# Even mixer's two borders: where the second stack, the gates' transposition, the context's norm and the late squares are issued

## The chip, the cores and the metric

The kernel runs on one core of one Trainium2 chip. The metric is device time in microseconds (us) of one execution, the median of several. The core's engines run side by side and each takes its own instructions in order: PE (TensorE) multiplies matrices and transposes, DVE (VectorE), ACT (ScalarE) and POOL (GpSimd) work on elements, and SP issues transfers from HBM.

## The reference

The program is a two-layer backbone over 256 context tokens and 256 latent tokens of width 1024. Layer 0 is a feed-forward, a mixer and a second feed-forward; layer 1 is the same with another mixer. The change lies in layer 0's ("even") mixer: differential attention with four heads beside a bidirectional mLSTM with four heads, which share one input and one output projection. Cut to what the change touches:

```python
def mlstm_scan(q, k, v, ig, lf, state):          # per direction, in chunks
        bcum = jnp.cumsum(fc, axis=-1)           # running sum of the log forget gates
        dmat = jnp.where(tril, bcum[..., :, None] - bcum[..., None, :] + ic[..., None, :], -jnp.inf)
        m_t = jnp.maximum(m_inter, jnp.max(dmat, axis=-1))
        s = jnp.einsum('bhtd,bhsd->bhts', qc, kc) * jnp.exp(dmat - m_t[..., None])
        num = jnp.einsum('bhts,bhse->bhte', s, vc) + ...
        h = num / jnp.maximum(jnp.abs(den), jnp.exp(-m_t))[..., None]

def ada_norm(x, g, shift, scale):                # ahead of every mixer and feed-forward
    return rms_norm(x, g) * (1.0 + scale) + shift

        x = x + mx[:, 5] * yx                    # residual behind the mixer, latents
        hctx = hctx + mc[5] * yc                 # and context
        x = x + 0.5 * mx[:, 8] * swiglu(ada_norm(x, norm_g[l, 2], mx[:, 6], mx[:, 7]), ...)
```

## The kernel before

Activations lie with features on the partitions: `xT[k]` is a 128 x 512 tile for each of eight feature blocks k, the context's 256 tokens (`CTX`) in the left half and the latents' (`LAT`) in the right. A float32 product is made of three matmuls on a high and a low half: `split` (L123) casts a weight tile to its high half `whi` on ACT (L120) and subtracts it on DVE to get `wlo` (L121). `whi` and `wlo` have two buffers each, so the third split waits until PE is through with the first. `mm_bank` gives one of two PSUM banks, `bank_m` and `bank_a` one of three each.

**The early border** (L733 to L790). Four tiles of mLSTM queries and keys `mq[0..3]` come out of `proj_first`. Behind them stands the gates' projection `psg`, 24 matmuls, and then a chain of small operations: L759 to L774 on DVE and ACT make the running sums and the gates `ga`, L775 and L776 split them into `gah` and `gal`, L778 to L781 make the running maximum `mst`. PE transposes it (L784, `pmt`), and DVE and ACT make `negm` and `em` of it. From there the four heads follow. Each head (`mlstm_head`, L919) takes two broadcasts of the gates (L805, `pA`), adds a mask (L807, `dg`), exponentiates on ACT (L824, L825), multiplies with scores from PE (L853, L854; L869 on DVE), scales (L881, L882), transposes the weights (L894, `pt`), multiplies them with the values (L907, `po`) and transposes the result (L916, `pt_o`).

The scores use a `stack` (L835): a pair of query and key tiles laid out in halves, with three casts on ACT (L843 to L845) and two subtractions on DVE (L846, L847) for each of its two parts. The first stack serves heads 0 and 1, the second heads 2 and 3. The values of all heads come from two calls of `proj_rows` (L620), each with 96 matmuls on two banks, each bank copied to `mv` on ACT when it is full (L636).

**The late border** (L1048 to L1060). The output projection makes its last four feature tiles (k = 4 to 7) first for the context, then for the latents in the order 6, 7, 4, 5. After each a `residual` updates `xT` (L296, DVE), and `stat` squares it (L255, ACT) and adds the square to `ssum` (L257, on POOL for latent tiles with k under 6, else on DVE). When all eight squares are in, PE sums over the partitions (L287, `ms`), ACT makes `rstd` (L263, L264), and `modulate` makes each of eight tiles: a product on DVE (L270), then for even k a cast on ACT (L277) and a low half on DVE (L278), for odd k two operations on ACT (L273, L274) and the low half on POOL (L275). The list `norm` holds the context's nine steps (factors, then k = 0 to 7); the loop issues them between the latents' products. The latents' norm follows inside the next feed-forward's `gemm_first` (L234), which starts with the context's product on the first weight tile (`ps_ab`).

**What sets the order.** The program is recorded in the order of the Python code, and a scheduler then places instructions on each engine, within data dependencies; it may move an instruction forward into a place where its engine would wait. So the code's order is not the engine's, and a single moved statement can move others. Buffers are given out in the scheduled order.

Of the kernel before, what the change touches and what calls it, by code (L numbers as in the profile page):

```python
# [34 lines left out]
def backbone_kernel(  # L35
# [213 lines left out]
    def stat(k, i, sl, apart=False):  # L249
        if k == 0:  # L250
            ssum[i] = [tp.tile([P, T], F32, tag=f"ssum{i}", name="ssum", bufs=1)]
            nc.scalar.square(ssum[i][0], xT[k][:, sl])
# [2 lines left out]
        nc.scalar.square(sq, xT[k][:, sl])  # L255
        if k < KC - 2 or not apart:
            (nc.gpsimd if i and k < KC - 2 else nc.vector).tensor_tensor(ssum[i][0], ssum[i][0], sq, ALU.add)  # L257
# [34 lines left out]
    def residual(k, ps, gate, i, sl, nxt):  # L292
        residual_at(k, ps[:, sl], gate, i, sl, nxt)

    def residual_at(k, o, gate, i, sl, nxt):
# [3 lines left out]
        stat(k, i, sl, nxt == (1, 2))  # L299
# [320 lines left out]
    def proj_rows(w, c0, dst, col):  # L620

        r3 = load(rows(w, c0, 256))
        ps = [mm_bank("ps_v") for _ in range(2)]
        for i in range(2):
            wh, wl = split(r3[:, 4 * i : 4 * i + 4])
            for t in range(4):
                o = ps[t // 2][:, (t % 2) * T : (t % 2) * T + T]
                for k4 in range(4):
# [5 lines left out]
                    nc.tensor.matmul(o, lhsT=al, rhs=wh[:, k4], start=False, stop=k == KC - 1 and t % 2 == 1)  # L634
        for a in range(2):
            nc.scalar.copy(dst[:, 2 * a : 2 * a + 2, col : col + T], ps[a].rearrange("p (t n) -> p t n", t=2))  # L636

# [42 lines left out]
    def even_mixer(nxt):  # L680
# [66 lines left out]
        psg = mm_bank("psg")  # L747
# [27 lines left out]
        nc.scalar.copy(gah, ga)  # L775
# [5 lines left out]
        nc.vector.tensor_tensor(mst[H2:P], mst[0:H2], bcum[0:H2], ALU.add)  # L781
        pmt = bank_m("pmt")
        for t in range(4):
            nc.tensor.transpose(pmt[:, t * P : t * P + P], mst[:, t * P : t * P + P], ident)  # L784
# [667 lines left out]
```

## Time and profile before

| what | value |
|---|---|
| median of 3 runs | 1802.88 us (1801.29 to 1802.92) |
| profiled execution, its own time | 1805.46 us |
| its span, first to last instruction | 1803.8 us |
| mean granted PE clock | 0.995 |
| PE busy from 430 to 445 us, and from 475 to 490 us | 15.00 and 14.95 of 15 us |
| PE busy from 600 to 640 us, and from 700 to 720 us | 40.00 of 40 and 20.00 of 20 us |

Times in rows are us from the span's start. The even mixer runs from about 400 to 671 us. A busy share over the whole span is an average over stages with different limits, so a stage is read from its own stretch: how long PE was busy in it, at what granted clock, and what ended PE's idle time. A row of the time order gives start, duration, engine, line, operation, what it writes and reads, and in brackets the idle time of its engine ahead of it with what ended it. Starts of matmuls lie closer than their durations, since they are pipelined; the pitch from start to start is what a matmul costs.

### The profile page before, as it was taken

The page shows a single profiled execution, that of the slowest core. Times are in us where ns is not written, and L with a number is a line of the kernel's source. Part 1 is how long each engine was busy: PE and PEld are TensorE (multiplying, and loading weights), DVE is VectorE, ACT ScalarE, POOL GpSimd, SP SyncE. Part 2 cuts the span into 40 slices and gives each one's busy share as a digit, 9 for nine tenths or more (in the row PEclk, how much of TensorE's full clock was granted, in tenths as well). Part 3 has the DMA queues.
Part 4 walks back from the last instruction along what each step waited for, and adds up shares of the span by engine and source line. Part 5 has one row for each costly group of instructions (what it writes and reads, how often), then busy time and mean ns, then how long its engine had stood idle before and what let it go on. Part 6 is the DMA issues. An engine that isn't in the chain of part 4 may idle for free.

```text
span 1803.8 us, 24901 instructions
## 1 busy us (share of the span) xinstructions
PE 1765.4 (98%) x10087; PEld 1503.6 (83%) x10087; DVE 1153.9 (64%) x1678; ACT 743.3 (41%) x1286; POOL 107.1 (6%) x172
## 2 busy tenths in 40 slices
PE   8999999999999999999999999999999999999998
PEld 5777778899887788777788897777888998899996
DVE  5767775657669866677753486777543747855555
ACT  4422222237658853222222352222222656654443
POOL 1000000013011020000000010000000200010000
PEclk9999999999999999999999999999999999999999
DMA  9555545443121214555542344555443632235553
GB/s 295 177 187 179 177 158 192 164 132 122 47 71 47 94 48 140 182 175 182 184 142 97 129 141 163 187 187 187 140 133 101 189 117 71 89 106 191 186 190 117
DMA packets 209303, 262.30 MB, mean 145 GB/s; under 512 B 6863, under 2 KB 188662, under 8 KB 209188
## 3 DMA queue, kind: packets, MB, share of 16 engines
q1 hardware_dynamic: 208160, 259.28, 44.0%
q8 instruction: 79, 1.29, 0.3%
q0 software_dynamic: 576, 0.84, 0.2%
q10 hardware_dynamic: 452, 0.59, 0.1%
q14 instruction: 36, 0.29, 0.1%
HBM read 259.64 MB, written 1.05 MB: 145 GB/s over the span
## 4 chain that ended last, share of the span: by engine, by line
PE 85%; DVE 7%; ACT 4%; issue 2%; DMA 1%; SPq 0%; POOL 0%; ACTq 0%; POOLq 0%; DVEq 0%
PE ps_ab L146 16%; PE ps_ab L147 16%; PE ps_ab L148 16%; PE ps_y L146 7%; PE ps_y L148 7%; PE ps_y L147 7%; PE ps_fm L148 2%; PE ps_fm L146 2%; PE ps_fm L147 2%; DVE wlo L121 1%; PE po L907 1%; PE ada_ps L190 1%; PE ps_l L1382 1%; PE ps_l L1383 1%; PE ps_l L1381 1%
## 5 line engine op out<-in xcount | busy, mean ns | idle before, releaser
L120 ACT CAST whi<-raw 128x1024 fp32r<-128x1024 f32 (+1 forms) x326 | 336.0, 1031 | 849.7 <-PE ps_ab L147 497.3
L121 DVE TENSOR_TENSOR wlo<-raw,whi 128x1024 fp32r<-128x1024 f32 (+1 forms) x326 | 392.6, 1205 | 314.4 <-ACT whi L120 309.5
L146 PE MATMUL ps_ab<-hh,whi 128*128 128x512 f32 (+1 forms) x1360 | 491.3, 362 | 1.8 <-ACT whi L120 1.0
L147 PE MATMUL ps_ab<-hl,whi 128*128 128x512 f32 (+1 forms) x1360 | 490.4, 361 | 2.6 <-POOL hl L275 2.3
L148 PE MATMUL ps_ab<-hh,wlo 128*128 128x512 f32 (+1 forms) x1360 | 489.4, 360 | 0.4 <-DVE wlo L121 0.3
L178 DVE SCALAR_TENSOR_TENSOR acc<-raw_ada,cs,acc 128x1024 f32<-128x1024 f32 x224 | 276.5, 1280 | 42.8 <-DMA raw_ada<-in_ada_w_dram 42.8
L146 PEld LDWEIGHTS ps_ab<-hh,whi 128*128 128x128 f32 x1360 | 255.4, 188 | 50.1 <-ACT whi L120 6.3
L147 PEld LDWEIGHTS ps_ab<-hl,whi 128*128 128x128 f32 x1360 | 255.9, 188 | 46.0 <-POOL hl L275 2.9
L148 PEld LDWEIGHTS ps_ab<-hh,wlo 128*128 128x128 f32 x1360 | 255.7, 188 | 44.0 <-DVE wlo L121 1.0
L148 PE MATMUL ps_y<-gh,wlo 128*128 128x512 f32 (+1 forms) x660 | 229.9, 348 | 0.4
L146 PE MATMUL ps_y<-gh,whi 128*128 128x512 f32 (+1 forms) x660 | 230.0, 348 | 0.0
L147 PE MATMUL ps_y<-gl,whi 128*128 128x512 f32 (+1 forms) x660 | 228.8, 347 | 0.0
L148 PEld LDWEIGHTS ps_y<-gh,wlo 128*128 128x128 f32 x660 | 124.9, 189 | 17.7 <-DVE wlo L121 1.6
L349 DVE TENSOR_TENSOR s<-ps_ab,s 128x512 f32<-128x512 f32 (+1 forms) x88 | 54.7, 623 | 132.6 <-PE ps_ab L148 131.1
L146 PEld LDWEIGHTS ps_y<-gh,whi 128*128 128x128 f32 x660 | 124.9, 189 | 17.1 <-ACT whi L120 1.2
L147 PEld LDWEIGHTS ps_y<-gl,whi 128*128 128x128 f32 x660 | 124.9, 189 | 15.5
L257 POOL TENSOR_TENSOR ssum<-ssum,sq 128x256 f32<-128x256 f32 x25 | 26.2, 1049 | 1117.8 <-ACT sq L255 842.2
L146 PE MATMUL ps_fm<-hh,whi 128*128 128x256 f32 (+1 forms) x256 | 83.8, 327 | 0.0
L148 PE MATMUL ps_fm<-hh,wlo 128*128 128x256 f32 (+1 forms) x256 | 83.2, 325 | 0.0
L147 PE MATMUL ps_fm<-hl,whi 128*128 128x256 f32 (+1 forms) x256 | 82.9, 324 | 0.0
L632 PE MATMUL ps_v<-whi,hh 128*128 128x256 f32 x256 | 73.4, 287 | 1.3 <-ACT mv L636 1.3
L633 PE MATMUL ps_v<-wlo,hh 128*128 128x256 f32 x256 | 73.9, 289 | 0.0
(375 smaller groups left out, 2383.4 us busy)
## 6 DMA issues: line engine op xcount, KB each, us to landing
raw<-in_ffn_w_in_dram SPq DMA_DIRECT2D x84, 1024.0 KB, 5.3
raw_ada<-in_ada_w_dram SPq DMA_DIRECT2D x64, 1024.0 KB, 5.0
raw<-in_ffn_w_out_dram SPq DMA_DIRECT2D x41, 1024.0 KB, 5.0
raw<-in_even_w_in_dram SPq DMA_DIRECT2D x12, 1024.0 KB, 5.3
raw<-in_odd_w_in_dram SPq DMA_DIRECT2D x12, 1024.0 KB, 5.4
raw<-in_ffn_w_out_dram SPq DMA_DIRECT2D x15, 768.0 KB, 4.3
raw_c<-in_ada_w_dram SPq DMA_DIRECT2D x16, 512.0 KB, 7.4
raw<-in_even_w_out_dram SPq DMA_DIRECT2D x4, 1024.0 KB, 5.0
```

The lines of the kernel that those rows point to most:

```text
L120: nc.scalar.copy(hi3, r3)
L121: eng.tensor_tensor(lo3, r3, hi3.bitcast(F32), ALU.subtract)
L146: nc.tensor.matmul(ps, lhsT=wh, rhs=ah, start=first, stop=False)
L147: nc.tensor.matmul(ps, lhsT=wh, rhs=al, start=False, stop=False)
L148: nc.tensor.matmul(ps, lhsT=wl, rhs=ah, start=False, stop=last)
L178: nc.vector.scalar_tensor_tensor(ada_acc[i], r3[:, k2], s, ada_acc[i], ALU.mult, ALU.add)
L190: nc.tensor.matmul(ps[32 * j : 32 * j + 32, :256], lhsT=unit_e[:, 2 * (n - first) + i], rhs=acc[i][:, j * 256 : j * 256 + 256], start=n == ...
L257: (nc.gpsimd if i and k < KC - 2 else nc.vector).tensor_tensor(ssum[i][0], ssum[i][0], sq, ALU.add)
L349: nc.vector.tensor_tensor(s[:, sl], ps[1][:, sl], s[:, sl], ALU.mult)
L632: nc.tensor.matmul(o, lhsT=ah, rhs=wh[:, k4], start=k == 0 and t % 2 == 0, stop=False)
L633: nc.tensor.matmul(o, lhsT=ah, rhs=wl[:, k4], start=False, stop=False)
L907: nc.tensor.matmul(po[:, t], lhsT=w[:, kt, (t % 2) * P : (t % 2) * P + P], rhs=v[:, kt, h * P : h * P + P], start=kt == 0, stop=kt == nk - 1,)
```

## The change

`behind` places one PE instruction after another one without a wait between them. The gates' accumulator `psg` moves from `mm_bank` to `bank_a`. `proj_rows` returns its matmuls, and the transposition's first one is placed behind the value matmul `values[1][7]`: the last of the 24 that the second call makes for its first bank's first half. The second stack's code is placed, on ACT and DVE, behind the cast of the gates (L775) and the end of their chain (L781). At the late border the context's norm is issued three steps after each of the first three latent tiles, where it was two, two, two and three; and `stat` takes the squares of latent tiles 4 and 5, the last two made, to DVE and those of 6 and 7 to POOL.

```diff
+    def behind(ins, first):
+        tc.add_manual_dep(
+            ins.ins, first.ins.name,
+            mybir.DependencyInfo(mybir.DependencyClass.NoSync, mybir.DependencyReason.DATA), reason="order",
+        )
...
-    def stat(k, i, sl, apart=False):
+    def stat(k, i, sl, apart=False, late=(KC - 2, KC - 1)):
...
-            (nc.gpsimd if i and k < KC - 2 else nc.vector).tensor_tensor(ssum[i][0], ssum[i][0], sq, ALU.add)
+            (nc.gpsimd if i and k not in late else nc.vector).tensor_tensor(ssum[i][0], ssum[i][0], sq, ALU.add)
...
-        psg = mm_bank("psg")
+        psg = bank_a("psg")
...
-        nc.scalar.copy(gah, ga)
+        gates_act = nc.scalar.copy(gah, ga)
...
-        nc.vector.tensor_tensor(mst[H2:P], mst[0:H2], bcum[0:H2], ALU.add)
+        gates_dve = nc.vector.tensor_tensor(mst[H2:P], mst[0:H2], bcum[0:H2], ALU.add)
...
-            nc.tensor.transpose(pmt[:, t * P : t * P + P], mst[:, t * P : t * P + P], ident)
+            to_columns = nc.tensor.transpose(pmt[:, t * P : t * P + P], mst[:, t * P : t * P + P], ident)
+            if t == 0:
+                gates_pe = to_columns
...
-        mlstm_head(0, lambda: rows_pair(2048, mv))
-        mstk.append(stack(mq[1], mq[3], ...))
+        values = []
+        mlstm_head(0, lambda: values.extend(rows_pair(2048, mv)))
+
+        behind(gates_pe, values[1][7])
+        with tc.issue_after(gates_act.ins), tc.issue_after(gates_dve.ins):
+            mstk.append(stack(mq[1], mq[3], ...))
...
-            residual(4 + t, p, gate, *STREAMS[1], nxt)
-            for f in norm[2 * n : 2 * n + 2] if n < 3 else norm[6:]:
+            residual(4 + t, p, gate, *STREAMS[1], nxt, late=(4, 5))
+            for f in norm[3 * n : 3 * n + 3]:
```

In the new file most lines have moved by 7 to 12: the cast of L120 is L127 there, the transposition of L784 is L795, the head's L894 is L906.

PE at the transposition `pmt`, before. `ps_v_3630` and `ps_v_3631` are the two banks of the first `proj_rows` call, `whi_3684` is its second split, `pA` the first head's broadcasts:

```order
L632 MATMUL ps_v_3631<-whi_3684,hh5_101 128x256
L633 MATMUL ps_v_3631<-wlo_3685,hh5_101 128x256
L634 MATMUL ps_v_3631<-whi_3684,hl5_109 128x256
L784 MATMUL pmt_3507<-ident_67,t1_3490 128x128 x4
L805 MATMUL pA_3534<-gahl_3485,oneh_3486 128x512
L805 MATMUL pA_3551<-gahl_3485,oneh_3486 128x512
L632 MATMUL ps_v_3631<-whi_3684,hh6_102 128x256
L633 MATMUL ps_v_3631<-wlo_3685,hh6_102 128x256
```

The same place now, with `whi_3742` the first split of the second call:

```order
L640 MATMUL ps_v_3740<-whi_3742,hh3_99 128x256
L641 MATMUL ps_v_3740<-wlo_3743,hh3_99 128x256
L643 MATMUL ps_v_3740<-whi_3742,hl3_107 128x256
L795 MATMUL pmt_3507<-ident_67,t1_3490 128x128 x4
L817 MATMUL pA_3534<-gahl_3485,oneh_3486 128x512
L817 MATMUL pA_3551<-gahl_3485,oneh_3486 128x512
L640 MATMUL ps_v_3741<-whi_3742,hh0_96 128x256
L865 MATMUL pS_3571<-stk2_3519,stk2_3518 128x256
```

The transposition has moved back from behind 78 value matmuls to behind 120, that is behind all 96 of the first call and 24 of the second. Between it and head 0's first weight transposition (L894) stood 64 value matmuls and stand 60; between head 1's L805 and its first L894 stood 35 wide matmuls of the next projection (`ps_fm`) and stand 41; ahead of head 1's L916 stood 19 of these and stand 7 with 35 value matmuls of the next pair. From head 3's L805 on PE's order is the old one.

ACT from the gates' last exponent to head 0, now (before, the casts of `stk2_3881`, `stk_3882` and `stk_3883` stood ahead of and between L760 to L762, and the copy of `ps_v_3630` ahead of L775):

```order
L773 ACTIVATE t1_3490<-t1_3490,one_t_86 64x512
L127 CAST whi_3742<-raw_3738 128x1024
L786 CAST gahl_3485<-ga_3484 64x512
L855 CAST stk2_3881<-mq1_3155 64x512
L856 CAST stk_3882<-mq3_3157 64x512
L857 CAST stk_3882<-mq3_3157 64x512
L646 COPY mv_3158<-ps_v_3630 128x2x256
L855 CAST stk2_3881<-mq1_3155 64x512
L856 CAST stk_3883<-mq3_3157 64x512
L857 CAST stk_3883<-mq3_3157 64x512
L646 COPY mv_3158<-ps_v_3631 128x2x256
L127 CAST whi_3794<-raw_3738 128x1024
```

The stack's six casts have moved behind the gates, and the value bank's copy with them. On DVE the end of the gates' chain now reads as follows, up to the first head's operands:

```order
L790 SCALAR_TENSOR_TENSOR t1_3490<-ga_3484 32x256
L128 TENSOR_TENSOR wlo_3743<-raw_3738,whi_3742 128x1024
L787 TENSOR_TENSOR gahl_3485<-ga_3484,gahl_3485 64x512
L791 SCALAR_TENSOR_TENSOR t1_3490<-ga_3484,t1_3490 32x256
L792 TENSOR_TENSOR t1_3490<-t1_3490,t2_3491 64x512
L858 TENSOR_TENSOR stk2_3881<-mq1_3155,stk2_3881 64x512
L859 TENSOR_TENSOR stk_3884<-mq3_3157,stk_3882 64x512
L858 TENSOR_TENSOR stk2_3881<-mq1_3155,stk2_3881 64x512
L859 TENSOR_TENSOR stk_3885<-mq3_3157,stk_3883 64x512
L128 TENSOR_TENSOR wlo_3795<-raw_3738,whi_3794 128x1024
L801 TENSOR_SCALAR negm_3512<-pmt_3507 128x32
```

A weight split has moved into the chain; four stack subtractions and a second split stand between its end (L792) and `negm`, where one subtraction and one split stood.

POOL at the late border, before. `ssum_5598` is the latents' sum, `sq_5879` and `sq_5917` the squares of tiles 4 and 5, `hl1` to `hl7` the context's low halves:

```order
L257 TENSOR_TENSOR ssum_5598<-ssum_5598,sq_5630 128x256
L275 TENSOR_TENSOR hl1_105<-u_5844,hh1_97 128x256
L275 TENSOR_TENSOR hl3_107<-u_5882,hh3_99 128x256
L257 TENSOR_TENSOR ssum_5598<-ssum_5598,sq_5879 128x256
L275 TENSOR_TENSOR hl5_109<-u_5920,hh5_101 128x256
L257 TENSOR_TENSOR ssum_5598<-ssum_5598,sq_5917 128x256
L275 TENSOR_TENSOR hl7_111<-u_5929,hh7_103 128x256
```

And now, with `sq_5804` and `sq_5846` the squares of tiles 6 and 7:

```order
L264 TENSOR_TENSOR ssum_5598<-ssum_5598,sq_5630 128x256
L264 TENSOR_TENSOR ssum_5598<-ssum_5598,sq_5804 128x256
L282 TENSOR_TENSOR hl1_105<-u_5815,hh1_97 128x256
L264 TENSOR_TENSOR ssum_5598<-ssum_5598,sq_5846 128x256
L282 TENSOR_TENSOR hl3_107<-u_5853,hh3_99 128x256
L282 TENSOR_TENSOR hl5_109<-u_5891,hh5_101 128x256
L282 TENSOR_TENSOR hl7_111<-u_5900,hh7_103 128x256
```

POOL's last two adds have moved ahead of the low halves of k = 3, 5 and 7. DVE at the same place now, from the last weight split on (`u_5896` and `u_5900` are the context's last two products):

```order
L128 TENSOR_TENSOR wlo_5955<-raw_5944,whi_5954 128x1024
L285 SCALAR_TENSOR_TENSOR hl4_108<-u_5858,md_112,hh4_100 128x256
L303 SCALAR_TENSOR_TENSOR xT4_92<-ps_y_5862,md_112,xT4_92 128x256
L277 SCALAR_TENSOR_TENSOR u_5896<-xT6_94,amp_113,rstd_5777 128x256
L277 SCALAR_TENSOR_TENSOR u_5900<-xT7_95,amp_113,rstd_5777 128x256
L264 TENSOR_TENSOR ssum_5598<-ssum_5598,sq_5888 128x256
L285 SCALAR_TENSOR_TENSOR hl6_110<-u_5896,md_112,hh6_102 128x256
L303 SCALAR_TENSOR_TENSOR xT5_93<-ps_y_5905,md_112,xT5_93 128x256
L128 TENSOR_TENSOR wspare_5989<-raw_5942,wspare_5987 128x512
L264 TENSOR_TENSOR ssum_5598<-ssum_5598,sq_5931 128x256
```

The two adds of squares (L264) are new here; three more splits of spares stand behind the last row.

More of the change, by code (lines that the diff above doesn't have):

```diff
@@ L290, in norm_steps, with residual, residual_at @@
         return [factors] + [lambda k=k: modulate(l, n, i, sl, k, rstd) for k in range(KC)]
-    def residual(k, ps, gate, i, sl, nxt):
-        residual_at(k, ps[:, sl], gate, i, sl, nxt)
-    def residual_at(k, o, gate, i, sl, nxt):
+    def residual(k, ps, gate, i, sl, nxt, **kw):
+        residual_at(k, ps[:, sl], gate, i, sl, nxt, **kw)
+    def residual_at(k, o, gate, i, sl, nxt, **kw):
         nc.vector.scalar_tensor_tensor(
@@ L298, in residual_at @@
         )
-        stat(k, i, sl, nxt == (1, 2))
+        stat(k, i, sl, nxt == (1, 2), **kw)
     def out_pass(pairs, streams, units, acts, bank, gate, nxt, between=()):
@@ L623, in proj_rows @@
         ps = [mm_bank("ps_v") for _ in range(2)]
+        done = []
         for i in range(2):
@@ L633, in proj_rows @@
                     nc.tensor.matmul(o, lhsT=ah, rhs=wl[:, k4], start=False, stop=False)
-                    nc.tensor.matmul(o, lhsT=al, rhs=wh[:, k4], start=False, stop=k == KC - 1 and t % 2 == 1)
+                    done.append(
+                        nc.tensor.matmul(o, lhsT=al, rhs=wh[:, k4], start=False, stop=k == KC - 1 and t % 2 == 1)
+                    )
         for a in range(2):
             nc.scalar.copy(dst[:, 2 * a : 2 * a + 2, col : col + T], ps[a].rearrange("p (t n) -> p t n", t=2))
+        return done
     def out_split(k, src, sl):
@@ L792, in rows_pair @@
         def rows_pair(c0, dst):
-            for i in range(2):
-                proj_rows(w_in, c0 + i * T, dst, i * T)
+            return [proj_rows(w_in, c0 + i * T, dst, i * T) for i in range(2)]
         def keys(t):
@@ L1009, in even_mixer @@
         mstk = [stack(mq[0], mq[2], half2 + slots1(("wTa2", 1), ("qk2", 1)), (nc.scalar.copy, nc.scalar.copy, nc.scalar.copy, nc.vector, nc.vector))]
-        mlstm_head(0, lambda: rows_pair(2048, mv))
-        mstk.append(stack(mq[1], mq[3], halves2("wTa4", 1) + slots1(("mq0", 1), ("mq2", 1), ("rsa", 1), ("qk3", 1)), (nc.scalar.copy, nc.scalar.copy, nc.scalar.copy, nc.vector, nc.vector)))
+        values = []
+        mlstm_head(0, lambda: values.extend(rows_pair(2048, mv)))
+        behind(gates_pe, values[1][7])
+        with tc.issue_after(gates_act.ins), tc.issue_after(gates_dve.ins):
+            mstk.append(stack(mq[1], mq[3], halves2("wTa4", 1) + slots1(("mq0", 1), ("mq2", 1), ("rsa", 1), ("qk3", 1)), (nc.scalar.copy, nc.scalar.copy, nc.scalar.copy, nc.vector, nc.vector)))
         mlstm_head(1, lambda: None)
```

## The prediction

> **What bounds the kernel now.** I read the page first. Its busy table says that TensorE is the engine to watch:
>
> ```profile
> PE 1765.4 (98%) x10087; PEld 1503.6 (83%) x10087; DVE 1153.9 (64%) x1678; ACT 743.3 (41%) x1286; POOL 107.1 (6%) x172
> ```
>
> PE is idle for 1803.8 - 1765.4 = 38.4 us of its span. No other engine comes near, so a change can win only idle PE time, or PE time at a lowered clock. The change touches the even mixer alone, so I then cut the span into stretches and looked at PE there. The columns are the stretch, its length, the busy time (and count) of PE, PEld, DVE, ACT and POOL, the granted clock, the DMA share and GB/s:
>
> ```profile
> 445.00:460.00 15.00, 10.43 (x72) 9.83 (x71) 12.10 (x18) 6.88 (x15) 0.52 (x1) 0.89 0.00 0
> 660.00:680.00 20.00, 17.57 (x131) 16.61 (x130) 15.84 (x29) 12.53 (x28) 6.14 (x6) 0.94 0.13 41
> 680.00:700.00 20.00, 20.00 (x165) 19.82 (x164) 16.57 (x23) 9.94 (x18) 3.74 (x4) 0.97 0.34 120
> ```
>
> Two places stand out. At 445 to 460 PE is idle for 15 - 10.43 = 4.57 us, and at 660 to 680 for 20 - 17.57 = 2.43 us. Each is followed by a lowered clock: lost clock time is (1 - 0.89) x 15 = 1.65 us at the first, and (1 - 0.94) x 20 + (1 - 0.97) x 20 = 1.8 us at the second. The first is the mixer's early border, where the gates are computed; the second is the late border, where the mixer's last projection hands over to the next feed-forward. Transfers bound neither (DMA share 0.00 to 0.34).
>
> PE's rows in order of time show the first (start, duration, then what ended an idle time):
>
> ```profile
> 441.32 0.28 PE L632 MATMUL ps_v<-whi,hh 128*128 128x256 f32 x1
> ...
> 446.88 0.27 PE L634 MATMUL ps_v<-whi,hl 128*128 128x256 f32 x1
> 448.43 0.39 PE L632 MATMUL ps_v<-whi,hh 128*128 128x256 f32 x1 [1.28 <-ACT mv L636]
> ...
> 455.54 0.79 PE L784 MATMUL pmt<-ident,t 128*128 128x128 f32 x4 [3.29 <-DVE t L781]
> ...
> 467.11 0.44 PE L894 MATMUL pt<-ident,E 128*128 128x128 f32 x2 [0.39 <-DVE E L882]
> ...
> 507.19 0.66 PE L916 MATMUL pt_o<-ident,on 128*128 128x128 f32 x4 [1.36 <-DVE on L913]
> ```
>
> Between the first two rows lie 48 value matmuls, so one takes (446.88 - 441.32) / 47 = 0.118 us. Then PE waits 1.28 us for ACT to empty a bank, and 3.29 us for the gates' last VectorE operation. The two waits make up the 4.57.
>
> **The early border, what goes.** ACT and DVE run the gates' chain, with the second stack's operations mixed in (L843 to L847):
>
> ```profile
> 441.81 1.28 ACT L107 ACT_TABLE_LOAD   x1
> ...
> 446.40 0.72 ACT L762 ACTIVATE t<-t,one_t 64x512 f32<-64x512 f32 x1
> 447.15 0.62 ACT L845 CAST stk<-mq 64x512 fp32r<-64x512 f32 x1
> 447.79 0.59 ACT L636 COPY mv<-ps_v 128x512 f32<-128x512 f32 x1
> 451.37 0.62 ACT L775 CAST gahl<-ga 64x512 fp32r<-64x512 f32 x1 [2.99 <-DVE ga L774]
> 451.90 1.04 ACT L120 CAST whi<-raw 128x1024 fp32r<-128x1024 f32 x1
> ```
>
> ```profile
> 447.16 0.68 DVE L763 TENSOR_TENSOR t<-t,t 64x512 f32<-64x512 f32 x1
> ...
> 454.80 0.69 DVE L781 TENSOR_TENSOR t<-t,t 64x512 f32<-64x512 f32 x1
> 455.51 0.69 DVE L847 TENSOR_TENSOR stk<-mq,stk 64x512 fp32r<-64x512 f32 x1
> 456.12 1.21 DVE L121 TENSOR_TENSOR wlo<-raw,whi 128x1024 fp32r<-128x1024 f32 x1
> 457.26 0.18 DVE L788 TENSOR_SCALAR negm<-pmt 128x32 f32<-128x32 f32 x1
> ...
> 466.58 1.54 DVE L882 SCALAR_TENSOR_TENSOR E<-E,den 128x256 f32<-128x256 f32 x3
> ```
>
> Two stack casts leave ACT ahead of the table load (2 x 0.62 = 1.24, so 440.5), and the three behind it that held up L762 go too (3 x 0.64 = 1.9). L762 so ends near 443.9, not 447.12. From L763's start to L781's end DVE takes 455.49 - 447.16 = 8.3 us; one weight split of 1.21 now stands inside. That gives 443.95 + 8.3 + 1.2 = 453.5 for the gates' end, 2 us sooner.
>
> PE does not use those 2 us. Its order puts 120 value matmuls ahead of the transposition, where 78 stood: 441.32 + 120 x 0.118 = 455.5, the same time as now. It gets there without a wait if its banks and splits are in time, and they are: the third split's cast waits for matmul 48 (447.0), ends at 448.1, and its subtraction stands on DVE to 451.3; the first bank, full at 441.32 + 72 x 0.118 = 449.8, is copied behind the gates' cast (448.8) and three stack casts, from 450.65 to 451.25; matmul 97 needs both at 452.65. With the gates' accumulator in another pool, nothing else holds a bank. So the waits of 1.28 and 3.29 us go, and the 1.65 of clock behind them: **6.2 us** off.
>
> **What comes instead.** The chain of head 0 does not get earlier. Behind L781 now stand four stack subtractions and a split on DVE before `negm`: 453.5 + 4 x 0.69 + 1.21 = 457.4, against 457.26 above. From there to the first L882 nothing on DVE or ACT is removed, so head 0's weights are ready at 467.2 as before. But PE has eaten its filler: behind the transposition (0.45) and L805 (0.48) stand 60 value matmuls (7.08) and six score matmuls (0.96), which ends at 464.5. PE waits 467.25 - 464.5 = 2.75 us where it waits 0.39: **2.4 us** given back, but with 42 matmuls (4.96 us) more behind it.
>
> Does that gap lower the clock? The trace has no gap of 2.75 us in one piece. Bounds: nothing, as behind the 1.28 and 1.36 above (the matmuls behind 448.43 are at 0.12 again), or 1.65, as behind 3.29. 2.75 is nearest to 3.29, so I take **1.65** and keep 0 as a rival. The Trainium skill, "TensorE: Matmul & The Clock Gate", Part 1, says that the clock is halved after an idle window of some 3.4 us; by it 2.75 us would cost nothing, though the trace shows the halving behind 3.29 already.
>
> In the later heads the filler between milestones shifts by a few matmuls. Head 1 shows it best:
>
> ```profile
> 481.91 0.70 PE L805 MATMUL pA<-gahl,oneh 128*128 128x512 f32 x2
> 482.42 1.29 DVE L807 TENSOR_TENSOR dg<-pA,tri 128x512 f32<-128x512 f32 x2 [0.98 <-PE pA L805]
> 491.66 0.38 PE L894 MATMUL pt<-ident,E 128*128 128x128 f32 x2
> ...
> 540.03 1.29 DVE L807 TENSOR_TENSOR dg<-pA,tri 128x512 f32<-128x512 f32 x2 [3.60 <-PE pA L805]
> ```
>
> The last row is head 3's. At head 1 a split now stands ahead of L807, whose cast waits for PE's last matmul of a tile. I make that 1.1 us of delay for the head's exponentials, against 41 - 35 = 6 wide matmuls more of filler, at twice the 0.118 each 1.4 us: no new wait. At head 1's end (507.19) there is 1.33 us more filler, but the chain also got later; I take 0.7 of the 1.36 off, and add 0.3 for other transpositions: **-0.4**, with bounds of -1.4 and +1.4. At head 3 the order joins the old one again, 5 us earlier, and from there DVE, ACT and PE have what they had. Early border in sum: -6.2 + 2.4 + 1.65 - 0.4 = **-2.6 us**, or -4.2 without the clock's drop.
>
> **The late border.** PE, ACT, POOL and DVE rows there, and the adds of squares by engine:
>
> ```profile
> 673.09 0.28 PE L148 MATMUL ps_ab<-hh,wlo 128*128 128x256 f32 x1
> ...
> 677.07 0.39 PE L147 MATMUL ps_ab<-hl,whi 128*128 128x256 f32 x1 [1.45 <-POOL hl L275]
> 677.29 0.28 PE L148 MATMUL ps_ab<-hh,wlo 128*128 128x256 f32 x1
> 677.41 0.68 PE L287 MATMUL ms<-ssum,ones_d 128*128 128x256 f32 x2
> ...
> 674.48 0.41 ACT L255 ACTIVATE sq<-xT 128x256 f32<-128x256 f32 x1
> 674.80 0.39 ACT L274 CAST hh<-u 128x256 fp32r<-128x256 f32 x1
> ...
> 675.03 0.85 POOL L257 TENSOR_TENSOR ssum<-ssum,sq 128x256 f32<-128x256 f32 x1 [2.25 <-ACT sq L255]
> 675.85 1.17 POOL L275 TENSOR_TENSOR hl<-u,hh 128x256 fp32r<-128x256 f32 x1
> ...
> 686.17 1.03 POOL L275 TENSOR_TENSOR hl<-u,hh 128x256 fp32r<-128x256 f32 x1 [0.52 <-ACT hh L274]
> ...
> 663.35 1.23 DVE L121 TENSOR_TENSOR wlo<-raw,whi 128x1024 fp32r<-128x1024 f32 x1 [0.48 <-ACT whi L120]
> ...
> 670.42 1.76 DVE L121 TENSOR_TENSOR wlo<-raw,whi 128x1024 fp32r<-128x1024 f32 x1
> 672.11 1.35 DVE L270 SCALAR_TENSOR_TENSOR u<-xT,amp,rstd 128x256 f32<-128x256 f32 x2
> ...
> L257 DVE TENSOR_TENSOR ssum<-ssum,sq x6: 411/424/426, 656.3 to 668.9; 128x256 f32<-128x256 f32 x6
> L257 POOL TENSOR_TENSOR ssum<-ssum,sq x2: 848/866/885, 670.2 to 675.0; 128x256 f32<-128x256 f32 x2
> ```
>
> Six matmuls stand between 673.09 and the `ms` of 677.41. At 0.117 us each `ms` would come at 673.9, so 3.5 us are lost, and 1.8 in clock. The last low half of the context waits on POOL behind an add, that on a square, and both on DVE's last context products at 672.11 to 673.46.
>
> In the new order the context's products come three to a step and two adds leave DVE's front. Walked with these durations: the last two products at 670.8 to 671.65 (1.8 us sooner), their cast ends at 672.55, and POOL, with its adds done, subtracts at once: 673.4 to 673.7. The last latent square ends at 673.4; its add stands on DVE behind one split of a spare (0.69) and ends at 674.2. PE needs the low half at 673.67 and `ms` at 673.9. I leave 0.7 us of wait, too short to lower the clock by the rows above: 3.5 + 1.8 - 0.7 = **4.6 us** off. Bounds: 5.3, with no wait, and 1.5, if the add slides behind all four spare splits (4 x 0.69 = 2.8 later, and the clock drops in part).
>
> One thing speaks against moving adds to DVE: beside POOL's reads the split of 1.23 took 1.76. The Trainium skill, "SBUF — State Buffer", section "Who interferes with whom", has the rule: a VectorE instruction with two SBUF inputs contends with a GpSimd one that reads SBUF. By it each add could stand up to 0.85 us more behind POOL, which would make the 4.6 some 3.8.
>
> Behind it the latents' norm has to keep up with PE: its last low half ends at 687.2, 9.8 us behind `ms`. PE first needs it behind 72 context and 21 latent matmuls, 93 x 0.117 = 10.9 us behind `ms`. With the same distance in the new order that leaves 1.1 us, so I cost it at nothing; without that cover each us later is a us of wait.
>
> **Sum.** The profiled execution took 1805.46 us (span 1803.8): 1805.46 - 2.6 - 4.6 = 1798.3. The runs' median lies 2.58 lower, so the forecast is **1795.7 us**.
>
> **Rivals.** (1) The clock stays up in the new gap: -4.2 - 4.6, 1794.0. For it: 1.36 us left it up; against: 3.29 did not, nor did 2.43 in pieces. The Trainium skill's rule on the clock, named above, ends at this time. (2) The early border nets nothing, because the heads, not PE, set the pace, and 42 matmuls less of filler come back as waits at L894 and L916: -4.6 alone, 1798.3. For it: PE's waits at 467.11 and 507.19 are for DVE; against: DVE itself idles for 3.60 us ahead of head 3's L807. (3) The late add slides: 3.1 less, 1798.8. (4) Both borders refill with waits: 1802.9. (5) Slower: each later head's split ahead of L807 delays its weights as head 0's are. It decides from the point where L807 is more than the 1.4 us of extra filler late; the price is 2.4 + 1.65 for each of three heads, 12 us: 1795.7 + 12 = 1807.8. My 1.1 for head 1 lies below that point, by little.
>
> **Chances.** Forecast 36%, rival 1 27%, rival 2 16%, rival 3 9%, rival 4 6%, rival 5 6%. The bound for a difference is 0.2%, about what a measurement here tells from none: 1799.3. Rivals 2 and 3 end just inside it and may fall on either side, so faster 0.83, same 0.11, slower 0.06. The range takes in the first four cases: 1792.0 (both borders with no new wait left) to 1799.6.
>
> **What would show it.** Right: no wait of PE at the transposition, a wait of 2 to 3 us at head 0's first L894 with a clock below 1.00 behind it, no wait over 1 us ahead of the late `ms`, and the clock at 1.00 in the stretch behind. Wrong: a wait at the value matmuls for a copy or a split, `negm` clearly after 457.4, waits of over 1 us at heads 1 and 2, or `ms` still held by the last add.

## The result and the profile after

The changed kernel takes 1794.11 us (median of 5, 1792.88 to 1796.81), the kernel before beside it 1802.92 us (median of 5, 1801.29 to 1806.45): a ratio of 0.9945, 95% interval 0.9934 to 0.9956 (the quotient of the two medians, 0.9951, lies inside it). The forecast was 1795.7 with a range of 1792.0 to 1799.6. The profiled execution is the one of 1792.88 us, with a span of 1791.2 us.

Busy line of the changed kernel's page. PE has 1757.3 us of work left where it had 1765.4, and 33.9 us of idle time where it had 38.4:

```profile
PE 1757.3 (98%) x10087; PEld 1497.5 (84%) x10087; DVE 1151.6 (64%) x1678; ACT 743.3 (41%) x1286; POOL 106.9 (6%) x172
```

Busy time by stretch, after (columns as in the prediction). The first row is the program's start, the others answer to the two places of the prediction:

```profile
0.00:50.00 50.00, 40.00 (x269) 29.03 (x270) 27.98 (x74) 20.78 (x43) 4.97 (x23) 1.00 1.07 298
445.00:460.00 15.00, 13.31 (x110) 12.88 (x109) 12.48 (x20) 10.49 (x22) 0.52 (x1) 1.00 0.18 54
460.00:475.00 15.00, 14.97 (x110) 13.72 (x109) 9.31 (x29) 10.34 (x26) 0.77 (x4) 1.00 0.24 72
660.00:680.00 20.00, 19.00 (x155) 18.33 (x155) 17.62 (x31) 13.32 (x29) 7.51 (x8) 1.00 0.31 107
680.00:700.00 20.00, 20.00 (x119) 17.53 (x118) 12.61 (x14) 7.68 (x10) 0.00 (x0) 1.00 0.47 157
```

PE is idle for 1.69 us in 445 to 460 (4.57 before) and for 1.00 in 660 to 680 (2.43 before), and the granted clock is 1.00 everywhere. The first row matters for reading totals: before, the same stretch ran at 0.93.

```profile
0.00:50.00 50.00, 41.81 (x255) 30.35 (x259) 27.23 (x73) 20.17 (x42) 4.99 (x23) 0.93 1.05 297
```

So the two profiles are some 2 us apart long before the change begins, and the two spans can't simply be subtracted. I measure the borders by two stretches that begin and end at the same instructions in every kernel: the **early stretch** from DVE's first read of `psg` to PE's first score of the attention's last unit, and the **late stretch** from there to ACT's table load behind the next feed-forward. PE's order differs between the two kernels only inside the early stretch. Their rows, before and after, in order of time:

```profile
441.80 0.76 DVE L759 TENSOR_SCALAR t<-psg,gb 64x512 f32<-64x512 f32 x1
...
614.27 0.28 PE L853 MATMUL pSa<-stk 128*128 128x256 f32 x1
...
929.89 1.28 ACT L107 ACT_TABLE_LOAD   x1
```

```profile
439.60 0.75 DVE L770 TENSOR_SCALAR t<-psg,gb 64x512 f32<-64x512 f32 x1 [1.31 <-PE psg L155]
...
605.72 0.28 PE L865 MATMUL pSa<-stk 128*128 128x256 f32 x1
...
918.16 1.28 ACT L114 ACT_TABLE_LOAD   x1
```

Early stretch: 614.27 - 441.80 = 172.47 us before, 605.72 - 439.60 = 166.12 after, **6.35 less**. Late stretch: 315.62 before, 312.44 after, **3.18 less**. Together 9.5, of which the medians show 8.8.

PE's rows with their waits in the changed kernel, in order of time (in brackets the idle time ahead and what ended it):

```profile
453.59 0.60 PE L795 MATMUL pmt<-ident,t 128*128 128x128 f32 x4
...
456.46 0.36 PE L865 MATMUL pS<-stk,stk 128*128 128x256 f32 x1 [1.69 <-DVE em L802]
...
464.65 0.41 PE L906 MATMUL pt<-ident,E 128*128 128x128 f32 x2
...
504.53 0.66 PE L928 MATMUL pt_o<-ident,on 128*128 128x128 f32 x4 [0.19 <-DVE on L925]
...
665.12 0.38 PE L154 MATMUL ps_ab<-hl,whi 128*128 128x256 f32 x1 [0.20 <-DVE hl L285]
...
666.24 0.39 PE L154 MATMUL ps_ab<-hl,whi 128*128 128x256 f32 x1 [0.42 <-POOL hl L282]
...
667.12 0.70 PE L294 MATMUL ms<-ssum,ones_d 128*128 128x256 f32 x2 [0.38 <-DVE ssum L264]
```

The transposition comes without a wait, as forecast. The new wait stands somewhere else than forecast: 1.69 us at head 0's first score matmul, for `em`, and none at its first weight transposition (464.65). Head 1's end waits 0.19 where it waited 1.36. DVE in the same place shows what `em` stood behind:

```profile
451.42 0.69 DVE L792 TENSOR_TENSOR t<-t,t 64x512 f32<-64x512 f32 x1
452.03 0.68 DVE L858 TENSOR_TENSOR stk<-mq,stk 64x512 fp32r<-64x512 f32 x1
...
454.89 1.23 DVE L128 TENSOR_TENSOR wlo<-raw,whi 128x1024 fp32r<-128x1024 f32 x1
456.04 0.18 DVE L801 TENSOR_SCALAR negm<-pmt 128x32 f32<-128x32 f32 x1
456.14 0.18 DVE L802 TENSOR_SCALAR em<-pmt 128x32 f32<-128x32 f32 x1
...
464.03 1.54 DVE L894 SCALAR_TENSOR_TENSOR E<-E,den 128x256 f32<-128x256 f32 x3
...
663.37 0.96 DVE L277 SCALAR_TENSOR_TENSOR u<-xT,amp,rstd 128x256 f32<-128x256 f32 x2
...
666.66 0.41 DVE L264 TENSOR_TENSOR ssum<-ssum,sq 128x256 f32<-128x256 f32 x1
```

The gates end at 452.11, then come four stack subtractions and a split, and only then `negm` and `em`. At the late border the context's last products now stand ahead of the adds, and the last add ends at 667.07, right ahead of `ms`.

### The profile page after: what moved, and what is told of

Same layout as the page of the kernel before. It is cut to its first block, busy times and chain, and to the rows that moved or that the text cites. A ratio compares the mean times of both kernels' runs of the same rounds, so it can differ in the third digit from the quotient of the medians.

```text
span 1791.2 us, 24909 instructions
## 1 busy us (share of the span) xinstructions
PE 1757.3 (98%) x10087; PEld 1497.5 (84%) x10087; DVE 1151.6 (64%) x1678; ACT 743.3 (41%) x1286; POOL 106.9 (6%) x172
## 3 DMA queue, kind: packets, MB, share of 16 engines
HBM read 259.64 MB, written 1.05 MB: 146 GB/s over the span
## 4 chain that ended last, share of the span: by engine, by line
PE 87%; DVE 7%; ACT 3%; issue 2%; DMA 1%; POOL 0%; SPq 0%; ACTq 0%; POOLq 0%; DVEq 0%
PE ps_ab L153 16%; PE ps_ab L154 16%; PE ps_ab L155 16%; PE ps_y L153 7%; PE ps_y L155 7%; PE ps_y L154 7%; PE ps_fm L155 2%; PE ps_fm L153 2%; PE ps_fm L154 2%; DVE wlo L128 1%; PE po L919 1%; PE ada_ps L197 1%; PE ps_l L1399 1%; PE ps_l L1400 1%; PE ps_l L1398 1%
## 5 line engine op out<-in xcount | busy, mean ns | idle before, releaser
L127 ACT CAST whi<-raw 128x1024 fp32r<-128x1024 f32 (+1 forms) x326 | 335.9, 1031 | 848.6 <-PE ps_ab L154 499.7
L264 POOL TENSOR_TENSOR ssum<-ssum,sq 128x256 f32<-128x256 f32 x25 | 26.7, 1070 | 1122.5 <-ACT sq L262 1121.9
```

Of the source, the lines that this page charges most:

```text
L127: nc.scalar.copy(hi3, r3)
L264: (nc.gpsimd if i and k not in late else nc.vector).tensor_tensor(ssum[i][0], ssum[i][0], sq, ALU.add)
```

## The experiments

Each kernel was profiled once, the one before twice, and each but the tied one was timed in several runs beside the kernel before. The stretches are the finer measure: where nothing is changed they repeat to 0.1 us from kernel to kernel, while a total moves by some us with the clock. "Slowed" names the border behind which the granted clock fell to 0.50 for about 3.4 us in that profile.

| kernel | early stretch | late stretch | slowed | ratio to before (95%) |
|---|---|---|---|---|
| before | 172.47 | 315.62 | both | |
| before, once more | 171.42 | 315.54 | late | one run, no ratio |
| changed | 166.12 | 312.44 | none | 0.9945 (0.9934 to 0.9956) |
| early border only | 166.12 | 314.09 | none | 0.9959 (0.9947 to 0.9972) |
| late border only | 172.42 | 312.46 | early | 0.9989 (0.9980 to 0.9999) |
| without the transposition's move | 170.64 | 312.42 | early | 0.9968 (0.9953 to 0.9983) |
| without the bank's move | 168.47 | 312.42 | none | 0.9963 (0.9948 to 0.9978) |
| without the stack's move | 166.27 | 312.45 | none | 0.9942 (0.9927 to 0.9956) |
| stack behind `em` | 165.99 | 312.46 | none | 0.9943 (0.9931 to 0.9956) |
| `pmt` in the other pool | 168.52 | 312.42 | early | 0.9963 (0.9950 to 0.9977) |
| the same, tied | 166.09 | 312.51 | none | one run, no ratio |
| without the sooner norm | 166.11 | 314.56 | late | 0.9963 (0.9948 to 0.9978) |
| without the late squares | 166.14 | 315.61 | late | 0.9962 (0.9950 to 0.9975) |

### Each border alone

The early border alone takes the late border's two edits back, the late border alone the early one's three:

```diff
-            residual(4 + t, p, gate, *STREAMS[1], nxt, late=(4, 5))
-            for f in norm[3 * n : 3 * n + 3]:
+            residual(4 + t, p, gate, *STREAMS[1], nxt)
+            for f in norm[2 * n : 2 * n + 2] if n < 3 else norm[6:]:
```

```diff
-        psg = bank_a("psg")
+        psg = mm_bank("psg")
...
-        behind(gates_pe, values[1][7])
-        with tc.issue_after(gates_act.ins), tc.issue_after(gates_dve.ins):
+        if True:
```

> Only the early border is changed (stack, transposition, gates' bank); the late border is as before. Theory A (read from the two traces: from the gates' first read of psg to the last projection's first matmul the changed kernel is 6.35 us shorter): 1802.9 - 6.35 = 1796.6, ratio 0.9965. Rival B (the prediction's own sum for this border): -2.6 with a clock drop, or -4.2 without: 1800.3 or 1798.7. Rival C (the two borders are not separate, the early gain is lost at the late border): 1802.9 within 1. In the profile A wants a wait of about 1.7 us of PE at head 0's first score matmul, for em, and none at the transposition.

> Only the late border is changed; the early one is as before. Theory A (from the traces: 3.19 us shorter from the last projection's first matmul to the next feed-forward's latent half): 1799.7, ratio 0.9982. Rival B (the prediction's sum, 3.5 + 1.8 - 0.7 = 4.6): 1798.3. A says that the 3.5 holds 1.1 us of slow clock that the 1.8 holds too, so that only 2.43 + 1.8 - 1.0 is there to win. In the profile A wants PE idle for about 1.0 us in the stretch that ends at ms, in two or three waits, and a clock of 1.00.

Both borders keep their own stretch to 0.1 us, so they are separate and add up. The early border gives the 6.35 that was read from the trace; its total (7.4 us, interval 5.1 to 9.6) rules out rivals B and C. The late one gives 315.62 - 312.46 = 3.16, theory A; its total (2.0 us, interval 0.2 to 3.6) holds A's 3.2 and leaves out the rival's 4.6. A's account of where the 4.6 went is another matter, and the last bullet on the prediction below corrects it. But the early border alone brought a surprise. Its late border is untouched, and it waits as before; PE's rows there, and two stretches:

```profile
664.66 0.39 PE L153 MATMUL ps_ab<-hh,whi 128*128 128x256 f32 x1 [0.30 <-ACT hh L284]
665.29 0.39 PE L154 MATMUL ps_ab<-hl,whi 128*128 128x256 f32 x1 [0.25 <-DVE hl L285]
...
666.23 0.39 PE L153 MATMUL ps_ab<-hh,whi 128*128 128x256 f32 x1 [0.43 <-ACT hh L281]
...
668.07 0.38 PE L154 MATMUL ps_ab<-hl,whi 128*128 128x256 f32 x1 [1.45 <-POOL hl L282]
```

```profile
664.00:669.00 5.00, 2.57 (x14) 1.70 (x13) 4.20 (x8) 3.65 (x8) 1.99 (x2) 1.00 0.05 9
669.00:672.00 3.00, 3.00 (x29) 3.00 (x28) 2.06 (x6) 2.30 (x6) 0.00 (x0) 1.00 1.07 362
```

The waits are 0.30, 0.25, 0.43 and 1.45, those of before to 0.01 us. But the clock behind them is 1.00, and the late stretch is 314.09 and not 315.62. The same waits don't always lower the clock.

### What lowers the clock

The kernel before was profiled once more, unchanged.

> The kernel before, unchanged, profiled once more. In its first profile PE's clock was at half speed for 3.42 us behind each of the two borders' waits; with the same four waits at the late border (0.30, 0.26, 0.43, 1.45 us) the run with the early border alone showed no drop. Theory A (the clock is set for one window of 3.41 us after another, on a grid that is fixed for a run and falls anywhere against the program; a window that was idle for about half or more halves the next): all ends of slow stretches of this run are equal modulo 3.413 us; the waits at both borders are as in the first profile within 0.03 us; behind the late border the clock drops only if one window holds both the 0.43 and the 1.45 us, which the grid read from the early border's drop tells. Rival B (the gap itself decides): the late border shows the drop again, 3.4 us long, whatever the grid.

This time the early border kept its clock and the late one lost it. Rival B fails: the same wait of 3.29 us lowered the clock in one profile and not in the other. The granted clock was at 0.50 from 455.92 to 459.34 and from 677.78 to 681.20 in the first profile of before, each 3.42 us long, and their ends lie 221.86 us apart, which is 65.0 times 3.413. In the second it was at 0.50 from 19.02 to 22.44 and from 674.38 to 677.80: 655.36 apart, 192.0 times 3.413. In every profile with two or more slow stretches ahead of its end (nine of them) the ends agree modulo 3.413 us to a few hundredths of it, and over the profiles that remainder lies anywhere from 0.11 to 0.99 of a window. So the clock is set window by window on a grid of 3.41 us, which falls anywhere against the program. Cut along that grid, the windows of before's first and second profile:

```profile
452.51:455.92 3.41, 0.38 (x3) 0.38 (x4) 3.27 (x6) 0.43 (x1) 0.52 (x1) 1.00 0.00 0
455.92:459.34 3.42, 3.42 (x17) 3.22 (x16) 2.81 (x6) 1.40 (x5) 0.00 (x0) 0.50 0.00 0
...
674.37:677.78 3.41, 1.53 (x8) 1.10 (x8) 2.74 (x4) 2.37 (x6) 1.98 (x2) 1.00 0.08 10
677.78:681.20 3.42, 3.42 (x18) 3.35 (x17) 2.39 (x6) 2.42 (x6) 0.00 (x0) 0.50 1.01 346
```

```profile
449.10:452.52 3.42, 1.80 (x16) 1.59 (x14) 3.31 (x5) 1.57 (x2) 0.00 (x0) 1.00 0.00 0
452.52:455.93 3.41, 1.74 (x13) 1.66 (x14) 3.31 (x6) 0.00 (x0) 0.52 (x1) 1.00 0.00 0
455.93:459.34 3.41, 3.41 (x28) 3.25 (x28) 1.79 (x7) 2.75 (x10) 0.00 (x0) 1.00 0.00 0
...
670.96:674.38 3.42, 1.28 (x5) 0.67 (x4) 2.62 (x6) 3.38 (x8) 1.75 (x2) 1.00 0.00 0
674.38:677.79 3.41, 3.12 (x12) 2.95 (x13) 1.80 (x4) 0.89 (x2) 0.23 (x1) 0.50 0.78 254
```

In the second profile the 3.29 us wait lay across two windows, which count 16 and 13 matmuls, and no slowing followed. In the first it lay in one, with 3 matmuls, and the next window ran at half clock. PE's idle time does not tell the two kinds apart as cleanly, as the run without the late squares shows: 

```profile
456.36:459.77 3.41, 1.72 (x13) 1.39 (x12) 3.35 (x7) 0.60 (x3) 0.00 (x0) 1.00 0.02 4
459.77:463.18 3.41, 3.41 (x29) 3.32 (x29) 1.23 (x6) 3.41 (x13) 0.00 (x0) 1.00 0.94 293
...
667.99:671.40 3.41, 1.78 (x9) 1.11 (x8) 2.61 (x4) 2.73 (x7) 2.06 (x2) 1.00 0.00 0
671.40:674.82 3.42, 3.42 (x17) 3.33 (x16) 2.52 (x7) 2.19 (x6) 0.00 (x0) 0.50 1.00 318
```

A window with 1.72 us busy and 13 matmuls is followed by full clock, one with 1.78 us busy and 9 matmuls by half. What does is the time that matmuls stream: starts times pitch, 0.118 us for 256 columns and 0.23 for 512. By this estimate (a 128-column transposition counted as half of 256 columns) the eight windows at the borders that were followed by slowing stream for 5 to 28% of their length. Of all other windows with more than 0.9 us of idle PE, between the first 30 us and PE's last matmuls, none was followed by slowing, and they stream for 38% or more. The first 30 us are left out, since matmuls have other shapes there. The estimate was fitted to these windows afterwards, and no run was built to test it. A matmul behind a wait counts as busy for 0.38 us where the others take 0.118, so several short waits starve a window more than their sum says.

What a slowing costs is read from a stretch with and without it. Half speed for 3.42 us would be 1.71 us. At the late border, with the same waits, it made 315.62 - 314.09 = 1.53. At the early one it made 172.47 - 171.42 = 1.05, since at full clock PE is sooner at a value bank and waits there, which it does not in the first profile:

```profile
462.11 0.39 PE L632 MATMUL ps_v<-whi,hh 128*128 128x256 f32 x1 [0.72 <-ACT mv L636]
```

### The early border's three parts

Each was undone alone: first the line `behind(gates_pe, values[1][7])` taken out, then `psg` put back into `mm_bank`, then the two `issue_after` taken from around the second stack.

> The changed kernel without the tie of the gates' transposition to the 128th value matmul; the order puts it behind 77 value matmuls again, ahead of 43. Stack and bank stay as changed. The measure is the stretch from the gates' first read of psg to the attention's first score of the last unit: 172.47 us before, 166.12 changed. Theory A (the place of the transposition is what takes PE's wait away): PE gets to it 4 to 5 us before the gates end (12.5 us behind the read of psg), waits 3.5 to 4.5 us there and about 1.7 us for em, and meets a lowered clock; the matmuls kept behind it win back 1 to 2 us at the heads: 169.5 to 172. Rival B (the stack's move is what counts, and filler kept is filler won): 166 to 168.5.

The early stretch is 170.64, theory A. PE waits at the transposition again, and again meets a lowered clock (0.50 from 452.66 to 456.08); that wait is shorter than I expected and there is none for `em`:

```profile
452.89 1.09 PE L795 MATMUL pmt<-ident,t 128*128 128x128 f32 x4 [2.88 <-DVE t L792]
```

> The changed kernel with the gates' accumulator psg back in the pool of the value banks. Same stretch (172.47 before, 166.12 changed). Theory A (psg holds the bank that the third value accumulator needs until ga is computed, 7.1 us behind the read of psg): PE waits 0.5 to 1.5 us at a value matmul, as the 1.28 us before, but the head's chain does not move, so that the wait at the scores gets shorter by the same: 166.1 to 166.6. Rival B (a wait at the values comes on top): 166.9 to 167.6.

168.47: more than either theory. PE's order is that of the changed kernel. Besides the wait for `ga`, which holds the bank, the order changed on ACT: a weight cast that stood ahead of the gates' cast stands behind five of the stack's casts, and PE then waits for that split:

```profile
449.70 0.36 PE L640 MATMUL ps_v<-whi,hh 128*128 128x256 f32 x1 [1.62 <-DVE ga L785]
...
457.77 0.39 PE L641 MATMUL ps_v<-wlo,hh 128*128 128x256 f32 x1 [2.03 <-DVE wlo L128]
```

> The changed kernel with the second stack issued where it was, in the middle of the gates' chain; transposition and bank stay as changed, and PE's order is the same word for word. Same stretch (172.47 before, 166.12 changed). Theory A (the stack's operations cost DVE the same time ahead of negm wherever they stand, since four subtractions and a split precede it either way): the gates end 2 us later, so PE waits 0.5 to 1.5 us at the transposition, em comes within 0.7 us of where it was, and the wait at the scores is shorter by what the first one took: 165.5 to 167. Rival B (the prediction's step: the stack's casts held up the gates' chain by 3.1 us on ACT, and that is what PE waited for): a wait of 2 us or more at the transposition and the wait of 1.7 us at the scores too, 168 or more.

166.27: theory A. The waits only divide differently, 0.90 + 0.91 = 1.81 where the changed kernel has 1.69:

```profile
456.83 0.66 PE L795 MATMUL pmt<-ident,t 128*128 128x128 f32 x4 [0.90 <-DVE t L792]
...
458.97 0.35 PE L865 MATMUL pS<-stk,stk 128*128 128x256 f32 x1 [0.91 <-DVE em L802]
```

So the transposition's place is worth some 4.5 us (1.0 to 1.7 of it clock), the bank's 2.35 with the changed order on ACT in it, and the stack's 0.15, nothing that a total could show. The three add up to 7.0 and not to 6.35, so they are not independent.

### What the new wait is worth

```diff
-        nc.vector.tensor_scalar(em, pmt4[:, :, 2:4, 0:4], -88.0, None, ALU.max)
+        em_dve = nc.vector.tensor_scalar(em, pmt4[:, :, 2:4, 0:4], -88.0, None, ALU.max)
...
-        with tc.issue_after(gates_act.ins), tc.issue_after(gates_dve.ins):
+        with tc.issue_after(gates_act.ins), tc.issue_after(em_dve.ins):
```

> The changed kernel with the second stack held behind em's VectorE operation, not behind the gates' last. Theory A (four stack subtractions of 0.7 us ahead of negm and em are the cause of the 1.69 us wait): em comes 2.8 us sooner, the wait at the scores goes, and the stack, first needed by head 2, fills DVE's idle time between head 0's exponentials: 1794.1 - 1.7 = 1792.4, ratio to before 0.9942. Rival B: the subtractions now delay head 0's weights by their 2.1 to 2.8 us, and the wait comes back at head 0's transposed weights: 1794.1 within 0.5, or up to 1 slower.

The wait of 1.69 is gone, so the subtractions did cause it. But 0.25 comes back at head 0's weights and 1.56 at head 1's end, and the stretch is 0.13 shorter, not 1.7: the wait moved, though to a place that rival B did not name. PE's order is the same up to head 0's first weights and differs at 170 places behind, so this run says less about what comes later.

```profile
466.12 0.41 PE L906 MATMUL pt<-ident,E 128*128 128x128 f32 x2 [0.25 <-DVE E L894]
...
505.93 0.66 PE L928 MATMUL pt_o<-ident,on 128*128 128x128 f32 x4 [1.56 <-DVE on L925]
```

```diff
-        pmt = bank_m("pmt")
+        pmt = bank_a("pmt")
```

> The changed kernel with the transposition's accumulator pmt in the other PSUM pool, so that head 0's first scores need not wait for em to read it. Theory A (the scores wait for pmt's bank; but head 0's exponentials need negm, which comes no sooner): the wait of 1.69 us leaves the scores and comes back at head 0's first transposed weights, as 1.2 to 1.9 us; time as the changed kernel, 1794.1 within 0.5. Rival B (the wait itself is the cost): 1.7 less, 1792.4, and no wait at the weights. Rival C (pmt's bank is not what the scores wait for): the wait of 1.7 stays ahead of the first score.

All three theories missed. The scheduler was free to move the two `pA` matmuls and the scores ahead of the transposition, and there `pA` waits 2.36 us for the gates' low half, with a slowed clock behind it. That answered another question than the one asked, so it was repeated with the order tied (the same for the first two scores):

```diff
-                nc.tensor.matmul(pA, lhsT=sel, rhs=gahl, start=True, stop=True)
+                got = nc.tensor.matmul(pA, lhsT=sel, rhs=gahl, start=True, stop=True)
+                if h == 0:
+                    behind(got, to_columns)
```

> As the run with pmt in the other PSUM pool, but with head 0's two pA matmuls and its first scores tied behind the transposition, where the changed kernel has them (there they had moved ahead of it and waited 2.36 us for the gates, so that it did not answer its question). Same stretch, from the gates' first read of psg to the attention's first score of the last unit (166.12 changed). Theory A (the scores waited for pmt's bank, and the head's chain is no sooner): no wait at the scores; PE gets to head 0's first transposed weights 1.7 us sooner and waits there 1.2 to 1.9 us; 165.9 to 166.4. Rival B (the wait itself was the cost): no wait at either, 164.2 to 164.8. Rival C (not pmt's bank): the wait of 1.7 stays at the scores.

```profile
461.70 0.50 PE L868 MATMUL pS<-stk,stk 128*128 128x512 f32 x1 [1.57 <-ACT E L838]
```

The wait at the first scores is gone: they had waited for `pmt`'s bank, the third of three. It comes back as 1.57 us, not at the weights but at the scores of the second unit, for the bank of a `pA` that ACT's exponentials still read. The stretch is 166.09. In all three runs that shorten or remove the wait of 1.69 (the stack's move undone, the stack behind `em`, this one) others of 1.6 to 1.8 us in sum come. Head 0's weights are ready 24.55, 23.89 and 24.36 us behind the first read of `psg`, 24.43 in the changed kernel. This fits a pace that the heads set; which part of head 0's chain sets it was not tested, and DVE itself waits there 2.18 us for PE's scores (460.03 in the changed kernel).

### The late border's two parts

Of the two lines shown for the late border, the first run takes back the loop over `norm`, the second the argument `late=(4, 5)`.

> The changed kernel with the late border's norm steps again two at a time; the last latent squares stay on VectorE. PE's order is the same. The measure is the stretch from the attention's last scores to the next feed-forward's table load on ACT: 315.62 us before with a slowed clock, 314.09 with the same waits and no slowing (early border alone), 312.44 changed. Theory A (POOL is free of an add of 0.85 us ahead of the last low half, but the context's last products stand where they stood): the wait of 1.45 shrinks to 0.5 to 0.9, PE idle 1.4 to 2.0 us in all, 313.1 to 313.7. Rival B (both parts are needed, one alone gives nothing): 314.0 or more.

> The changed kernel with the last latent squares added on POOL again; the norm steps stay three at a time. PE's order is the same. Same stretch (314.09 without slowing and without the late change, 312.44 changed). Theory A (the sooner norm is the part that counts; in this order POOL makes the last low halves first and its add of 0.85 us ends no later than VectorE's 0.41 behind a spare split): PE idle 0.9 to 1.5 us, 312.3 to 312.9. Rival B (the adds on POOL hold ms, the sum over squares, by another 0.5 us or more): 312.95 to 313.6. Rival C (one part alone gives nothing): 314.0 or more.

Both fell into a slowed window. Less its cost of 1.5 to 1.7 us, an estimate from the pair above and from 3.42 us at half speed, they would be near 312.9 to 313.0 and 313.9 to 314.1. The first is below A's 313.1 to 313.7, the second is far above A's 312.9 and at C. The waits say why. Without the sooner norm:

```profile
667.59 0.38 PE L153 MATMUL ps_ab<-hh,whi 128*128 128x256 f32 x1 [0.77 <-ACT hh L281]
...
668.62 0.39 PE L154 MATMUL ps_ab<-hl,whi 128*128 128x256 f32 x1 [0.65 <-POOL hl L282]
```

and without the late squares:

```profile
669.91 0.39 PE L154 MATMUL ps_ab<-hl,whi 128*128 128x256 f32 x1 [0.62 <-POOL hl L282]
...
671.04 0.90 PE L294 MATMUL ms<-ssum,ones_d 128*128 128x256 f32 x2 [0.62 <-POOL ssum L264]
```

With the squares on POOL the last add ends behind the last low half, and `ms` waits 0.62 for it; I had it end no later than VectorE's. By this estimate the sooner norm alone gives 0.2 us or nothing and the late squares alone some 1.1 to 1.2, and the two together 314.09 - 312.44 = 1.65. Their larger use is another: in all eight profiles with both parts the late border was not slowed, and in four of the five that lack one or both it was.

## Why the prediction was right

The sign, the places and the total were right (-8.8 us against -7.2), but by the case of rival 1, an unslowed clock, and by two sums that were off in opposite directions: the early border gave 3.75 us more than forecast and the late one 1.4 less. That the total comes out 1.6 us from the forecast is in part luck. Step by step:

- **The gates end 2 us sooner, and PE does not use it.** They end 452.11 - 439.60 = 12.51 us behind the first read of `psg`, 13.69 before: 1.2 sooner. So `negm` came 456.04 - 439.60 = 16.4 behind it, where the forecast had 457.4 - 441.8 = 15.6; a later `negm` was a sign named for being wrong. That PE does not use it was right, and the run without the stack's move shows it to the end.
- **6.2 us off at the values and the transposition.** Both waits went. The 1.65 of clock in it was there in only two of the three profiles with the old early border (172.47 and 172.42, against 171.42 without slowing), and made 1.05 there. Without it the early border removes 171.42 - 166.12 = 5.3.
- **2.75 us of new wait at the first L894.** The mechanism held: head 0's weights come little sooner, 464.03 - 439.60 = 24.4 us behind `psg`, 24.8 before. (In before's second profile, without slowing, it is 23.7, so the slow clock had held up that chain too.) The place and the size did not. PE came 0.3 later to the transposition (453.59 - 439.60 = 13.99, forecast 13.7), needed 9.37 us and not 9.0 from there to L894, and its first weights' transposition came 0.4 sooner (25.05 behind `psg`, forecast 25.45): 2.75 - 0.3 - 0.4 - 0.4 = 1.7. And since `pmt` holds one of three banks until `em` is read, the wait fell ahead of the filler and not behind it. I had not counted banks there.
- **1.65 of clock in that gap.** This step failed. The clock was 1.00. The argument took a gap's length for the cause, where the profiles point to the emptiest window of a fixed grid. A wait of 1.69 alone can empty only half a window.
- **-0.4 in the later heads.** Mis-sized. Behind head 0's weights and up to head 2's end PE waited 1.36 + 0.45 + 0.22 + 0.23 = 2.26 before and 0.21 + 0.19 + 0.23 = 0.63 after, 1.6 less. The filler that was used up early was not missed there.
- **4.6 at the late border.** It gave 3.2. The 3.5 was right: four waits of 2.44 us in sum, and 4 x (0.39 - 0.117) = 1.1 for the four matmuls that stood alone behind them. It holds none of the slow clock that the expectation for the late border alone put into it: the clock fell at 677.78, behind `ms` (677.41), and with the early border alone, at full clock, `ms` was as late (668.41 - 664.08 = 4.33 us behind the same matmul, 677.41 - 673.09 = 4.32 before). What was mis-sized is the 0.7 left. PE lost 1.8 there, 1.00 in three waits and 0.8 in the matmuls behind them, because the context's last products ended 1.2 us later against PE than forecast (at 664.33, 0.2 us ahead of the matmul at 664.53 that answers to the one at 673.09, where the forecast had 1.4), and `ms` did wait 0.38 for the last add, another sign named for being wrong. And the 1.8 of clock made 1.53: 3.5 - 1.8 + 1.5 = 3.2. The fear of adds beside POOL did not come true, they took 0.41 each; but three of the context's products took 2.24 (658.79) where POOL worked on a low half and an add, and 1.27 before where POOL was idle (664.82).

In sum the early border gave 6.35 where I had 2.6, the late one 3.2 where I had 4.6. Without any slowing the two are 5.3 + 1.65 = 7.0, with both windows slowed 9.5; the measured 8.8 lies between. Rival 2 (the heads set the pace) fits head 0, where removed waits returned, but not for the whole border, since the 42 matmuls of filler did fill time that PE had lost. Rivals 3, 4 and 5 did not occur. What stays open: which share of the 8.8 is clock, since only one profile of each kernel shows the grid, and where between 28% and 38% of streaming the clock falls.

## What to carry to other kernels

Fill a wait with work whose place is free before shortening the chain that ends it: the moved transposition was worth 4.5 us, and in the three runs that took the next wait away it only moved. The delay of a milestone is more than the waits ahead of it: here 3.5 us held 2.4 of idle time and 1.1 of matmuls that stood alone, and what is left after a change has both parts again. Price a slowed clock by the same stretch with and without it: 1.05 and 1.53 us here, not 1.7. A total that varies by a few us may hold clock slowings that come and go between runs, so compare stretches between the same two instructions, and look at the granted clock in each.

## What was not expected of the hardware

PE's granted clock falls to 0.50 for whole windows of 3.41 us, on a grid that is fixed within a run and differs between runs; at the two borders a window in which matmuls stream for 5 to 28% of the time, by the estimate above, was followed by one at half clock, and a window with 38% or more was not. The Trainium skill, "TensorE: Matmul & The Clock Gate", Part 1, speaks of an idle window of some 3.4 us; the length agrees, but a window with 10 matmuls and 1.80 us of busy PE (665.98 to 669.39 without the sooner norm) was enough to lower the clock here. The same happens in the first 30 us of the program: two slow windows in some runs, one or none in others, which puts some 2 us between two profiles of kernels that are alike there (0.93 and 1.00 in the rows of the first 50 us).
